# One encoder layer: convolution statistics placed a chunk later, channel sums behind the first key projection, nine gate tiles in the last head pair, and another order of the first output products

## The chip, the cores and the metric

The program runs on one core of one Trainium2 chip. The metric is the device time of one execution in microseconds (us); the median of several runs is compared. The core has TensorE (PE, matrix products), VectorE (DVE), ScalarE (ACT), GpSimd (POOL) and SyncE (SP, which issues most DMAs). Each engine works through its own list of instructions in order and waits on semaphores for what another engine or a DMA has to finish first. TensorE's clock is granted at one of two levels, 1.2 or 2.4 GHz; a granted clock of 0.50 in a view is the lower one.

## The reference, cut to what matters

All inputs are fp32; the width D is 1024. There are 16 meta tokens, 512 prompt tokens and 1024 sample tokens. The two batches are computed together, 1536 tokens beside the meta tokens.

```python
def encoder_layer(h, ...):                 # h: (1, 16 + T, 1024)
    u = rms_norm(h, pre_g)
    z = einsum('bld,de->ble', u, w_in)     # 7 x 1024 output columns
    c_val, c_glu, c_gate, q, k, v, a_gate = split(z)
    conv_out = conv_module(c_val, c_glu, ...) * silu(c_gate)
    o_meta, o_grid = neighbourhood_attention(q, k, v, ..., rel_bias)   # 16 heads of 64
    att = concatenate([o_meta, o_grid]) * silu(a_gate)
    mixed = concatenate([conv_out, att], axis=-1)                      # 2048 channels
    y = einsum('ble,ed->bld', mixed, w_out)
    return h + rms_norm(y, post_g)

def conv_module(val, glu_gate, conv_w, conv_b, ln_g, ln_b):
    u = val * sigmoid(glu_gate)
    y = depthwise_conv(u, conv_w)          # 31 taps along the tokens, per channel
    y = layer_norm(y + conv_b, ln_g, ln_b) # over the 1024 channels of a token
    return silu(y)
```

## The kernel before, in words

**Products.** Every fp32 product is made of three: an operand is split into a high part and the remainder (`whi`, `wlo` for weights, `uw` tiles for tokens), and each contraction chunk gives hi·hi, lo·hi and hi·lo. A projection of 128 output channels over 512 tokens (`proj`, L179) is one PSUM tile of 24 matmuls. A weight block is loaded by SP, cast on ACT (L140) and subtracted on POOL (L141), one block ahead of its use.

**Order.** The program is written as one stream; a scheduler in the framework then sets the order on each engine, by its own simulated times, and pools of buffers add waits. Within an engine that order is fixed.

**Stages.** First the pre-norm with its transposes. Then the convolution stage: the 1024 channels are eight chunks of 128. For chunk c, ACT makes the sigmoid of the glu tiles (L237), DVE multiplies the value tiles into `ub` (L254; one of the two buffers `ub0`, `ub1`), three small copies on POOL (L249, L260, L261) fill the 15-column edges between the token segments, ACT makes the first tap (L267: bias and one scaled copy), and DVE adds the other 30 taps (`conv_taps`, L269), each over 128 x 1536. Chunk 0's taps are made segment by segment as its tokens arrive. From chunk 0 a pivot `m0` per token is taken (`conv_mean`, three ones-matmuls at L279). The statistics of a chunk (`conv_stats`, three parts of 512 tokens) are: `zc` = z - m0 on DVE (L286), its square `zq` on ACT (L291, one buffer), and two running sums on POOL, `acc` (L292) and `accsq` (L293). The centred `zc` goes to DRAM.

**What TensorE does meanwhile.** The table `FILL` gives, per chunk, the fill units beside the next chunk's glu and value tiles: `v` is one unit of value projection (24 matmuls of 256 columns), `c3` or `a1` three tiles of a convolution or attention gate (`c_gate`, `a_gate`; each evacuated by an ACT copy to `ag`, L352, and stored). `TAP_US` is the time that the code allots to a tap when it interleaves the two streams of code, `TAP_MEAN` the tap of chunk 1 behind which `conv_mean` is coded.

**After the convolution.** Six ones-matmuls (L460) sum `acc` and `accsq` over the channels into `std` in DRAM; each result passes through an ACT copy (L462). Then `pair_proj(0)` (four tiles of keys, evacuated on ACT and DVE, L519 to L528) and `pair_q(0,0)`. `e_build` loads the bias tables and adds the masks on POOL (L541). Eight head pairs follow, each in six groups: scores (L602), softmax, transposes (L624), weighted values (L640). `between` puts a projection between two groups; in the last pair, which has no next pair to project for, it takes gate tiles of pairs 4 and 5. Behind the last pair stand the six tiles of `a_gate(6, 7)`.

**Output.** `mix(t, part)` builds the normalized, gated operand of 128 tokens (part 0 convolution, part 1 attention) from DRAM: loads `mb`, `mx`, `gt`, DVE and ACT arithmetic (on ACT a table load, the root L744, eight scaled silus L760, the gate's silu L761, the cast L763). `load_wo(n)` loads and splits block n of 16 of the output weights. The products `py` (L781) of the first two token tiles run side by side over n, then ten more tiles one by one.

## Time and profile before

| what | us |
|---|---|
| runs | 1496.85, 1497.6, 1500.35 |
| median | 1497.6 |
| the profiled execution | 1499.63 |
| its span, first to last instruction | 1497.9 |
| granted clock of TensorE, mean | 0.983 |

The span runs from the first instruction to the last; the execution's time has 1.73 us more around it. Stages in the profile's clock: pre-norm and first projections to about 80, convolution stage to 655, sums and first keys to 696, eight pairs to 1185, the last gates to 1220, output projection to the end.

### The profile page before, as it was taken

The page shows a single profiled execution, that of the slowest core. Times are in us where ns is not written, and L with a number is a line of the kernel's source. Part 1 is how long each engine was busy: PE and PEld are TensorE (multiplying, and loading weights), DVE is VectorE, ACT ScalarE, POOL GpSimd, SP SyncE. Part 2 cuts the span into 40 slices and gives each one's busy share as a digit, 9 for nine tenths or more (in the row PEclk, how much of TensorE's full clock was granted, in tenths as well). Part 3 has the DMA queues.
Part 4 walks back from the last instruction along what each step waited for, and adds up shares of the span by engine and source line. Part 5 has one row for each costly group of instructions (what it writes and reads, how often), then busy time and mean ns, then how long its engine had stood idle before and what let it go on. Part 6 is the DMA issues. An engine that isn't in the chain of part 4 may idle for free.

```text
span 1497.9 us, 24017 instructions
## 1 busy us (share of the span) xinstructions
PE 1450.2 (97%) x9506; PEld 1244.1 (83%) x9506; DVE 1008.5 (67%) x1707; ACT 592.6 (40%) x1297; POOL 339.7 (23%) x260
## 2 busy tenths in 40 slices
PE   7999799999999998989999999999999889999998
PEld 6988698898998887868888888888888668888886
DVE  7599999898989898943555566555555572634341
ACT  7312111212111211123554455555555584566650
POOL 1034351514231414141211111111111001221220
PEclk9999899999999999999999999999999699999999
DMA  8113231222222122232122222122222592545441
GB/s 275 28 42 86 65 92 43 86 79 74 91 82 63 63 83 63 93 100 57 59 61 72 67 72 73 48 73 64 76 76 70 162 305 83 163 145 172 126 136 43
DMA packets 124469, 138.90 MB, mean 93 GB/s; under 512 B 8110, under 2 KB 96430, under 8 KB 124356
## 3 DMA queue, kind: packets, MB, share of 16 engines
q1 hardware_dynamic: 124356, 137.36, 30.0%
q8 instruction: 74, 1.21, 0.4%
q14 instruction: 39, 0.32, 0.1%
HBM read 99.05 MB, written 42.71 MB: 95 GB/s over the span
## 4 chain that ended last, share of the span: by engine, by line
PE 50%; DVE 22%; POOL 3%; DMA 2%; ACT 2%; issue 2%; SPq 0%; DVEq 0%; ACTq 0%; POOLq 0%
DVE z L269 21%; PE mm L179 20%; PE py L781 18%; PE ss L602 5%; PE po L640 4%; PE tp L624 3%; POOL acc L292 2%; DMA mx<-zs 1%; DMA wraw<-in_wo 1%; POOL accsq L293 1%; ACT z L267 1%; ACT mx L760 0%; POOL wlo L141 0%; DMA cgd<-ag 0%; DVE zc L286 0%
## 5 line engine op out<-in xcount | busy, mean ns | idle before, releaser
L179 PE MATMUL mm<-uw,whi 128*128 128x512 f32 (+2 forms) x1888 | 548.4, 370 | 2.6 <-ACT ag L462 1.6
L269 DVE SCALAR_TENSOR_TENSOR z<-ub,cw_sb,z 128x1536 f32<-128x1536 f32 (+2 forms) x270 | 513.4, 1913 | 39.3 <-ACT z L267 31.5
L179 PEld LDWEIGHTS mm<-uw,whi 128*128 128x128 f32 x1888 | 340.0, 190 | 59.7 <-ACT ag L462 3.1
L179 PE MATMUL mm<-uw,wlo 128*128 128x512 f32 (+2 forms) x944 | 348.2, 369 | 2.9 <-POOL wlo L141 2.9
L141 POOL TENSOR_TENSOR wlo<-wraw,whi 128x1024 fp32r<-128x1024 f32 x48 | 134.2, 2797 | 388.8 <-ACT whi L140 374.1
L179 PEld LDWEIGHTS mm<-uw,wlo 128*128 128x128 f32 x944 | 179.3, 190 | 29.5 <-POOL wlo L141 3.3
L781 PE MATMUL py<-uw,mh 128*128 128x512 f32 x576 | 178.6, 391 | 0.0
L179 PE MATMUL tp<-uw,whi 128*128 128x512 f32 (+2 forms) x528 | 142.0, 352 | 0.0
L781 PEld LDWEIGHTS py<-uw,mh 128*128 128x128 f32 x576 | 108.1, 188 | 23.5
L613 ACT ACTIVATE pt<-pt,sm 128x216 f32<-128x216 f32 (+4 forms) x192 | 97.3, 507 | 73.5 <-DVE sm L612 71.9
L781 PE MATMUL py<-uw,ml 128*128 128x512 f32 x288 | 112.6, 391 | 0.0
L764 POOL TENSOR_TENSOR ml<-mx,mh 128x1024 fp32r<-128x1024 f32 x20 | 50.5, 2540 | 241.7 <-ACT mh L763 241.7
L179 PEld LDWEIGHTS tp<-uw,whi 128*128 128x128 f32 x528 | 93.3, 188 | 13.6
L626 ACT COPY pT<-tp 108x256 f32<-108x256 f32 (+4 forms) x192 | 79.3, 423 | 63.6 <-PE tp L624 55.2
L609 DVE CUSTOM_DVE_ANT_0 pt<-ss,ei 128x216 f32<-128x216 f32 (+2 forms) x144 | 62.6, 438 | 59.9 <-PE ss L602 46.4
L179 PE MATMUL tp<-uw,wlo 128*128 128x512 f32 (+2 forms) x264 | 93.0, 352 | 0.0
L624 PE MATMUL tp<-ident,pt 128*96 128x128 f32 (+2 forms) x480 | 89.3, 281 | 1.2 <-ACT pT L626 0.9
L757 DVE TENSOR_TENSOR mx<-mx,mb 128x1024 f32<-128x1024 f32 x12 | 14.7, 1224 | 107.3 <-DMA mx<-zs 107.3
L291 ACT ACTIVATE zq<-zc 128x512 f32<-128x512 f32 x24 | 15.2, 632 | 177.3 <-DVE zc L286 131.8
L332 PE MATMUL mm<-vh,uw 128*128 128x256 f32 x448 | 83.9, 284 | 0.8 <-ACT uw L204 0.6
L615 DVE TENSOR_SCALAR pt<-pt,sm 128x216 f32<-128x216 f32 (+4 forms) x192 | 79.9, 418 | 5.4
L614 DVE RECIPROCAL sm<-sm 128x1 f32<-128x1 f32 x192 | 31.3, 163 | 69.4 <-ACT pt L613 66.8
(184 smaller groups left out, 2335.3 us busy)
## 6 DMA issues: line engine op xcount, KB each, us to landing
wraw<-in_w_main SPq DMA_DIRECT2D x48, 512.0 KB
xt<-in_xn SPq DMA_DIRECT2D x12, 512.0 KB
vd<-vs SPq DMA_DIRECT2D x96, 64.0 KB
zs<-zc SPq DMA_DIRECT2D x24, 256.0 KB
...
```

The costliest lines, as they stand in the source:

```text
L141: eng.tensor_tensor(out=lo, in0=raw, in1=hi.bitcast(F32), op=ALU.subtract)
L179: last_mm[0] = nc.tensor.matmul(ps[:, :n], lhsT=w[:, dc, :], rhs=u[dc // 4][:, dc % 4, :], start=(dc == 0 and i == 0), stop=(dc == DC - 1 ...
L269: nc.vector.scalar_tensor_tensor(out=zv, in0=ub[:, a:b, k:k + 512], scalar=cw_sb[:, c, k:k + 1], in1=zv, op0=ALU.mult, op1=ALU.add)
L332: nc.tensor.matmul(ps[:, :256], lhsT=u[dc // 4][:, dc % 4, :], rhs=w[dc // 4][:, dc % 4, :], start=(dc == 0 and i == 0), stop=(dc == DC - ...
L602: last_qk[0] = nc.tensor.matmul(ss[:, :nk * w], lhsT=q[:, jj].rearrange("p h x -> p (h x)"), rhs=k[:, b0:b0 + nk, ra:ra + rn, :].rearrange ...
L609: nc.vector.tensor_tensor_reduce(out=pv.rearrange("p (k x) -> p k x", k=nk), in0=sv_, in1=e.rearrange("p k r c -> p k (r c)"), scale=1.0, ...
L613: last[0] = nc.scalar.activation(out=pv, in_=pv, func=AF.Exp, bias=sm[:, 1:2], scale=1.0, accum_out=sm[:, 2:3])
L615: nc.vector.tensor_scalar(out=pv, in0=pv, scalar1=sm[:, 3:4], scalar2=None, op0=ALU.mult)
L624: nc.tensor.transpose(out=tp[:kt, k * 128:k * 128 + 128], in_=pv[:, k * kt:k * kt + kt], identity=ident)
L626: nc.scalar.copy(out=pT[:kt, :nt * 128], in_=tp[:kt, :nt * 128])
L640: last_pv[0] = nc.tensor.matmul(po[hs, j, :], lhsT=v, rhs=pT[:kt, k * 128 + h * 64:k * 128 + h * 64 + 64], start=(k == 0), stop=(k == nt - ...
L781: nc.tensor.matmul(pss[hf], lhsT=m[e // 8][:, e % 8], rhs=w[e][:, hf * 512:hf * 512 + 512], start=(n == 0 and i == 0), stop=(n == 15 and i ...
```

## The change

1. `FILL` is dealt out anew: chunk 0's stretch gets five `v` units, later ones seven rather than eight, and the attention gate `a3` leaves the convolution stage. `TAP_US` becomes 2.3 and `TAP_MEAN` 14.
2. The statistics of chunk c-1 are coded behind taps 4, 8 and 12 of chunk c (for c = 1 behind taps 17, 21 and 25). Those of chunk 7 are coded behind its taps, with their sums on DVE.
3. The three edge copies of `ub` go from POOL to ACT.
4. The six channel sums (now L538) are coded behind `pair_proj(0)` and `pair_q(0,0)` and use the `ss` and `tp` banks; the pools and memsets that need the space of the convolution move with them.
5. `between` of the last pair takes nine gate tiles (`a3`, `a4`, `a5`) rather than six.
6. In the output part `mix(0,(1,))`, `mix(1,(0,))` and `mix(1,(1,))` are coded behind weight blocks 5, 7 and 9, the second of them held behind the last gate copy. The first two token tiles multiply the convolution half (n = 0 to 7) of tile 0, then of tile 1, then the attention halves.

```diff
-TAP_US = 1.85
-TAP_MEAN = 6
+TAP_US = 2.3
+TAP_MEAN = 14
-FILL = ("", "v5 c0 v3", "v8 c1", "v1 c2 v7", "v5 c3 v3", "v8 c4", "v1 c5 c6", "a0 a1 a2 a3 c7")
+FILL = ("v5", "c0 v7", "v5 c1 v2", "v7 c2", "v3 c3 v4", "v7 c4", "v1 c5 c6", "a0 a1 a2 c7")
...
-                nc.gpsimd.tensor_copy(out=ub[:, 1, 527:542], in_=ub[:, 2, 15:30])
-                nc.gpsimd.tensor_copy(out=ub[:, 2, 0:15], in_=ub[:, 1, 512:527])
+                nc.scalar.copy(out=ub[:, 1, 527:542], in_=ub[:, 2, 15:30])
+                nc.scalar.copy(out=ub[:, 2, 0:15], in_=ub[:, 1, 512:527])
...
+        first = TAP_MEAN + 3 if c == 1 else 4
         for k, _ in enumerate(conv_taps(c, z, 0, 3)):
             yield TAP_US
             if c == 1 and k == TAP_MEAN:
                 with tc.issue_after(last_mm[0]):
                     conv_mean(zprev[0])
-            if c == 1 and k == TAP_MEAN + 3:
-                for i in range(3):
-                    conv_stats(0, zprev[0], i, nc.gpsimd)
-                    yield TAP_US / 3
-        for i in range(3):
-            conv_stats(c, z, i, nc.gpsimd)
-            yield TAP_US / 3
+            if k in (first, first + 4, first + 8):
+                conv_stats(c - 1, zprev[0], (k - first) // 4, nc.gpsimd)
+                yield TAP_US / 3
+        if c == 7:
+            for i in range(3):
+                conv_stats(c, z, i, nc.vector)
...
+    for _ in pair_proj(0):
+        pass
+    pair_q(0, 0)
     for i in range(3):
         sl = slice(i * 512, i * 512 + 512)
         for k, src in enumerate((acc, accsq)):
-            ps = new_mm()
+            pool, tag = ((ps_s, "ss"), (ps_t, "tp"))[k]
+            ps = pool.tile([128, 512], F32, name=tag, tag=tag)
...
-        for p in (4, 5):
+        for p in (3, 4, 5):
             yield from a_gate(p)
...
         elif p == NPAIR - 1:
-            next(rest, None)
+            for _ in range(1 if i == 1 else 2):
+                next(rest)
...
+        if n == len(groups) + 1:
+            next(rest)
         if n >= 2:
             with tc.issue_after(last_qk[0].ins):
                 weighted(*groups[n - 2])
+        if n == len(groups):
+            next(rest)
...
     for n in range(16):
-        if n == 2:
-            mix(1, (0,))
+        if n == 6:
             mix(0, (1,))
+        elif n == 8:
+            with tc.issue_after(last_copy[0]):
+                mix(1, (0,))
+        elif n == 10:
             mix(1, (1,))
         load_wo(n)
...
-    for n in range(16):
+    for part in range(2):
         for t in range(2):
-            for hf in range(2):
-                product(t, together[t], n, hf)
+            for n in range(part * 8, part * 8 + 8):
+                for hf in range(2):
+                    product(t, together[t], n, hf)
```

**ScalarE between chunk 2 and chunk 3.** A row is a line, an operation and its tiles (`sg` the sigmoid, `zq` the squares, `z` the first tap, `vh` and `whi` casts of weights). Before:

```order
L237 ACTIVATE sg_2351<-tp 128x512
L140 CAST whi<-wraw 128x1024
L291 ACTIVATE zq<-zc 128x512 x3
L267 ACTIVATE z<-ub_129,cb_sb,cw_sb 128x1536
L140 CAST vh<-wraw 128x1024
```

In the changed kernel, at the same boundary (lines are shifted by one):

```order
L140 CAST whi<-wraw 128x1024
L250 COPY ub_129<-ub_129 128x15
L292 ACTIVATE zq<-zc 128x512
L262 COPY ub_129<-ub_129 128x15
L292 ACTIVATE zq<-zc 128x512 x2
L140 CAST whi<-wraw 128x1024
L261 COPY ub_129<-ub_129 128x15
L268 ACTIVATE z<-ub_129,cb_sb,cw_sb 128x1536
```

The three squares still stand ahead of the first tap (L267, now L268), and the edge copies stand among them. So it is also at the boundary from chunk 4 to 5; at the other four, the third square stands behind the first tap, as here from chunk 3 to 4:

```order
L250 COPY ub_128<-ub_128 128x15
L262 COPY ub_128<-ub_128 128x15
L292 ACTIVATE zq<-zc 128x512 x2
L261 COPY ub_128<-ub_128 128x15
L268 ACTIVATE z<-ub_128,cb_sb,cw_sb 128x1536
L292 ACTIVATE zq<-zc 128x512
```

**VectorE at the end of the convolution stage.** `kl` and `ql` are the low parts of keys and queries. Before:

```order
L254 TENSOR_TENSOR ub_129<-tp,sg_4724 128x8x8x8
L269 SCALAR_TENSOR_TENSOR z<-ub_129,cw_sb,z 128x1536 x30
L286 TENSOR_TENSOR zc<-z,m_987 128x512 x3
L520 TENSOR_TENSOR kl<-mm,kh 128x8x8 x2
L528 TENSOR_TENSOR kl<-mm,kh 128x4x64 x2
```

Now:

```order
L287 TENSOR_TENSOR zc<-z,m_987 128x512 x3
L255 TENSOR_TENSOR ub_129<-tp,sg_4718 128x8x8x8
L270 SCALAR_TENSOR_TENSOR z<-ub_129,cw_sb,z 128x1536 x30
L287 TENSOR_TENSOR zc<-z,m_987 128x512 x3
L293 TENSOR_TENSOR acc<-acc,zc 128x512 x2
L294 TENSOR_TENSOR accsq<-accsq,zq 128x512
L293 TENSOR_TENSOR acc<-acc,zc 128x512
L294 TENSOR_TENSOR accsq<-accsq,zq 128x512
L498 TENSOR_TENSOR kl<-mm,kh 128x8x8
L294 TENSOR_TENSOR accsq<-accsq,zq 128x512
L498 TENSOR_TENSOR kl<-mm,kh 128x8x8
L506 TENSOR_TENSOR kl<-mm,kh 128x4x64 x2
```

The evacuation of the first key tiles (L498, L506) stands behind the taps of chunk 7 and all its sums but the last. The 30 taps are still one unbroken run: the `zc` of chunk 6 were coded among them, and the scheduler put them ahead, where they stood before; it does so with the statistics of chunks 1 to 5 too.

**ScalarE around the last gate copy.** `uw`, `whi` are places that the output weights' high parts take, `mh0` to `mh2` the high parts of the mixed operand. Before:

```order
L352 COPY ag_11994<-mm_11969 128x512
L732 CAST uw_12161<-wraw_12159 128x1024
L760 ACTIVATE mx_12041<-mx_12041,lb_sb_97,lg_sb_96 128x128 x8
L732 CAST uw_12166<-wraw_12164 128x1024
L352 COPY ag_12022<-mm_11997 128x512
L763 CAST mh2_12056<-mx2_12049 128x1024
```

Now:

```order
L353 COPY ag_11994<-mm_11969 128x512
L744 CAST uw_12160<-wraw_12158 128x1024
L744 CAST uw_12171<-xr_12169 128x1024
L744 CAST uw_12176<-yo_12174 128x1024
L353 COPY ag_12022<-mm_11997 128x512
L756 ACT_TABLE_LOAD
L756 ACTIVATE mb_12044<-mb_12044,eps_sb_89 128x128
```

The last gate copy stood behind the eight silus of `mix(1,(0,))` and one weight cast; now it stands behind three weight casts, and that `mix` follows it.

## Rows read from the trace of the kernel before

**Rows 1.** The page's first lines: the span, and each engine's busy time, share of the span and instructions.

```profile
span 1497.9 us, 24017 instructions
PE 1450.2 (97%) x9506; PEld 1244.1 (83%) x9506; DVE 1008.5 (67%) x1707; ACT 592.6 (40%) x1297; POOL 339.7 (23%) x260
```

**Rows 2.** The page's 40 slices of 37.4 us: busy tenths of PE, and the clock granted to TensorE in tenths.

```profile
PE   7999799999999998989999999999999889999998
PEclk9999899999999999999999999999999699999999
```

**Rows 3.** The page's chain of work that ended last: shares of the span by engine, then by line.

```profile
PE 50%; DVE 22%; POOL 3%; DMA 2%; ACT 2%; issue 2%; SPq 0%; DVEq 0%; ACTq 0%; POOLq 0%
DVE z L269 21%; PE mm L179 20%; PE py L781 18%; PE ss L602 5%; PE po L640 4%; PE tp L624 3%; POOL acc L292 2%; DMA mx<-zs 1%; DMA wraw<-in_wo 1%; POOL accsq L293 1%; ACT z L267 1%; ACT mx L760 0%; POOL wlo L141 0%; DMA cgd<-ag 0%; DVE zc L286 0%
```

**Rows 4.** Waits of PE, and one of DVE: who waits, for whom, us in total, times, the longest.

```profile
PE ss L279 <- DVE z L269: 8.0, 1, 8.0
PE py L781 <- ACT ag L352: 5.7, 1, 5.7
...
DVE z L269 <- ACT z L267: 31.5, 6, 7.1
```

**Rows 5.** Timeline of DVE between chunk 2 and chunk 3: start, length, instruction, and in brackets the idle time before it and who ended it.

```profile
273.74 1.81 DVE L269 SCALAR_TENSOR_TENSOR z<-ub,cw_sb,z 128x1536 f32<-128x1536 f32 x1
275.64 3.00 DVE L286 TENSOR_TENSOR zc<-z,m 128x512 f32<-128x512 f32 x3
278.56 1.28 DVE L254 TENSOR_TENSOR ub<-mm,sg 128x512 f32<-128x512 f32 x2
286.00 17.27 DVE L269 SCALAR_TENSOR_TENSOR z<-ub,cw_sb,z 128x1536 f32<-128x1536 f32 x5 [6.17 <-ACT z L267]
```

**Rows 6.** Timeline of POOL there.

```profile
276.41 3.38 POOL L292 TENSOR_TENSOR acc<-acc,zc 128x512 f32<-128x512 f32 x2 [6.57 <-DVE zc L286]
279.75 1.29 POOL L293 TENSOR_TENSOR accsq<-accsq,zq 128x512 f32<-128x512 f32 x1
281.00 1.29 POOL L292 TENSOR_TENSOR acc<-acc,zc 128x512 f32<-128x512 f32 x1
282.24 0.20 POOL L261 COPY ub<-ub 128x15 f32<-128x15 f32 x1
282.39 1.28 POOL L293 TENSOR_TENSOR accsq<-accsq,zq 128x512 f32<-128x512 f32 x1
```

**Rows 7.** Timeline of ACT there.

```profile
276.42 0.63 ACT L291 ACTIVATE zq<-zc 128x512 f32<-128x512 f32 x1 [17.96 <-DVE zc L286]
281.07 0.63 ACT L291 ACTIVATE zq<-zc 128x512 f32<-128x512 f32 x1 [4.02 <-POOL accsq L293]
283.70 0.63 ACT L291 ACTIVATE zq<-zc 128x512 f32<-128x512 f32 x1 [1.99 <-POOL accsq L293]
284.24 1.66 ACT L267 ACTIVATE z<-ub,cb_sb,cw_sb 128x1536 f32<-128x1536 f32 x1
```

**Rows 8.** Taps beside POOL: timeline of DVE and of POOL between chunk 1 and chunk 2, and one piece of the chain of waits, in chunk 3, beside a subtraction of POOL's L141.

```profile
210.75 15.77 DVE L269 SCALAR_TENSOR_TENSOR z<-ub,cw_sb,z 128x1536 f32<-128x1536 f32 x6
208.60 6.15 POOL L292 TENSOR_TENSOR acc<-acc,zc 128x512 f32<-128x512 f32 x3
299.44 3.85 DVE z L269
```

**Rows 9.** Timeline of PE behind its wait for a weight block, and of ACT at two gate tiles that follow each other at the full clock.

```profile
586.33 0.79 PE L179 MATMUL mm<-uw,wlo 128*128 128x512 f32 x1 [2.95 <-POOL wlo L141]
600.11 0.59 ACT L352 COPY ag<-tp 128x512 f32<-128x512 f32 x1 [4.88 <-PE tp L179]
605.55 0.59 ACT L352 COPY ag<-tp 128x512 f32<-128x512 f32 x1 [4.85 <-PE tp L179]
```

**Rows 10.** The end of the convolution stage: timelines of DVE (the last two taps, the `zc` of chunk 7; and a lone `zc` of chunk 0), POOL (the last sum) and PE (the first score).

```profile
645.03 3.67 DVE L269 SCALAR_TENSOR_TENSOR z<-ub,cw_sb,z 128x1536 f32<-128x1536 f32 x2
648.73 2.99 DVE L286 TENSOR_TENSOR zc<-z,m 128x512 f32<-128x512 f32 x3
137.65 0.68 DVE L286 TENSOR_TENSOR zc<-z,m 128x512 f32<-128x512 f32 x1
659.62 1.26 POOL L293 TENSOR_TENSOR accsq<-accsq,zq 128x512 f32<-128x512 f32 x1 [0.74 <-ACT zq L291]
695.76 0.29 PE L602 MATMUL ss<-kh,qh 128*128 128x264 f32 x1
```

**Rows 11.** Two of the sums on PE (line's instructions: duration in ns min/median/max, first and last start; a sum is two matmul records).

```profile
L460 PE MATMUL tp<-acc,ones x2: 592/592/592, 656.5 to 657.0; 128*1 128x512 f32 x2
```

**Rows 12.** Busy time by stretch: the stretch, its length, busy time of PE, PEld, DVE, ACT and POOL, the granted clock, the DMA share and GB/s. The last pair's end and the stretch before the first output products.

```profile
1162.00:1166.00 4.00, 1.95 (x13) 1.58 (x13) 1.78 (x9) 1.38 (x4) 0.00 (x0) 0.94 1.11 313
1166.00:1189.20 23.20, 18.72 (x165) 14.75 (x164) 12.62 (x32) 18.97 (x35) 0.00 (x0) 0.50 0.21 69
1219.00:1226.00 7.00, 1.27 (x6) 0.73 (x5) 5.57 (x6) 5.64 (x12) 0.00 (x0) 0.83 1.03 380
1226.00:1230.00 4.00, 4.00 (x10) 3.13 (x11) 2.66 (x5) 3.39 (x4) 0.00 (x0) 0.50 1.01 287
```

**Rows 13.** Timeline of ACT: the silus of `mix` in the last pair and ahead of the last gate copy.

```profile
1178.30 3.18 ACT L760 ACTIVATE mx<-mx,lb_sb,lg_sb 128x128 f32<-128x128 f32 x8
1220.46 3.18 ACT L760 ACTIVATE mx<-mx,lb_sb,lg_sb 128x128 f32<-128x128 f32 x8 [0.72 <-DVE mx L758]
```

More of the change, by code (lines that the diff above doesn't have):

```diff
@@ L73, in _plan @@
         seq += [32 + p, 24 + p]
-    return chunks, seq + [40 + p for p in range(4, NPAIR)]
+    return chunks, seq + [40 + p for p in range(3, NPAIR)]
 CONV_ORDER = tuple((k, i) for k in "gv" for i in range(4))
@@ L218, in tile_encoder @@
     es1 = ExitStack()
-    vpool = es1.enter_context(tc.tile_pool(name="vpool", bufs=1, side="right", reuse_waits="tile"))
+    es1v = ExitStack()
+    vpool = es1v.enter_context(tc.tile_pool(name="vpool", bufs=1, side="right", reuse_waits="tile"))
     cpool = es1.enter_context(tc.tile_pool(name="cpool", bufs=1, reuse_waits="tile"))
@@ L248, in value @@
                     nc.vector.tensor_tensor(out=ub[:, 0, 0:15], in0=psv[:, 1:16], in1=sg[:, 1:16], op=ALU.mult)
-                    nc.gpsimd.tensor_copy(out=ub[:, 1, 0:15], in_=ub[:, 0, 0:15])
+                    nc.scalar.copy(out=ub[:, 1, 0:15], in_=ub[:, 0, 0:15])
                     continue
@@ L351, in gates @@
                 gt = gpool.tile([128, 512], F32, name="ag", tag="ag", bufs=2)
-                nc.scalar.copy(out=gt, in_=ps)
+                last_copy[0] = nc.scalar.copy(out=gt, in_=ps).ins
                 nc.sync.dma_start(dst[g][c], gt)
@@ L453, in tile_encoder @@
             pass
-    for i in range(3):
-        sl = slice(i * 512, i * 512 + 512)
-        for k, src in enumerate((acc, accsq)):
-            ps = new_mm()
-            nc.tensor.matmul(ps[0:1], lhsT=ones[:, 0:1], rhs=src[:, sl], start=True, stop=True)
-            row = gpool.tile([128, 512], F32, name="ag", tag="ag", bufs=2)
-            nc.scalar.copy(out=row[0:1], in_=ps[0:1])
-            nc.sync.dma_start(std[k:k + 1, sl], row[0:1])
-    es1.close()
+    es1v.close()
     banks[:] = 0, ((ps_mm, "mm"),)
     es2 = ExitStack()
-    apool = es2.enter_context(tc.tile_pool(name="apool", bufs=1, reuse_waits="tile"))
     kpool = es2.enter_context(tc.tile_pool(name="kpool", bufs=1, side="right", reuse_waits="tile"))
@@ L473, in tile_encoder, with new_qb @@
     qbs = []
-    for i in range(3):
-        pool = qpool if i < 2 else apool
+    def new_qb(pool):
+        i = len(qbs)
         qh = pool.tile([128, 4, 2, 64], F32R, name=f"qh{i}")
@@ L481, in tile_encoder @@
         qbs.append((qh, ql))
[L482 to L497 removed]
+    for _ in range(2):
+        new_qb(qpool)
     qcount = [0]
@@ L562, in pair_q, with e_build @@
             qbuf[p, g, hf] = qh, ql
+    for _ in pair_proj(0):
+        pass
+    pair_q(0, 0)
+    for i in range(3):
+        sl = slice(i * 512, i * 512 + 512)
+        for k, src in enumerate((acc, accsq)):
+            pool, tag = ((ps_s, "ss"), (ps_t, "tp"))[k]
+            ps = pool.tile([128, 512], F32, name=tag, tag=tag)
+            nc.tensor.matmul(ps[0:1], lhsT=ones[:, 0:1], rhs=src[:, sl], start=True, stop=True)
+            row = gpool.tile([128, 512], F32, name="ag", tag="ag", bufs=2)
+            nc.scalar.copy(out=row[0:1], in_=ps[0:1])
+            nc.sync.dma_start(std[k:k + 1, sl], row[0:1])
+    es1.close()
+    apool = es2.enter_context(tc.tile_pool(name="apool", bufs=1, reuse_waits="tile"))
+    new_qb(apool)
+    ebufs = []
+    for g in range(3):
+        R, mr = GR[g]["R"], META_ROW[g]
+        ei = apool.tile([128, 3, R, 8], F32, name=f"ei{g}")
+        ne = 3 if g == 0 else 2
+        e0 = apool.tile([128, ne, R, 8], F32, name=f"e0{g}")
+        e7 = apool.tile([128, ne, R, 8], F32, name=f"e7{g}")
+        nc.gpsimd.memset(ei[:, 0:2, mr, :], 0.0)
+        nc.gpsimd.memset(ei[:, 2, mr, :], NEG)
+        k7 = ne - 2
+        nc.gpsimd.memset(e0[:, 0:2, mr, :], 0.0)
+        nc.gpsimd.memset(e7[:, k7:k7 + 2, mr, :], 0.0)
+        if g == 0:
+            nc.gpsimd.memset(e0[:, 2], NEG)
+            nc.gpsimd.memset(e7[:, 0], NEG)
+        ebufs.append((ei, e0, e7))
+    def e_build(p):
+        for var in range(3):
+            raw = apool.tile([128, 15, 24], F32, name="raw", bufs=2)
+            nc.sync.dma_start(raw.rearrange("p i c -> p (i c)"), ed[var, 2 * p:2 * p + 2].rearrange("h r q n -> (h r q) n"))
+            for g in range(3):
+                r0, n, i0 = GROWS[g]
+                e = ebufs[g][var]
+                nk = 3 if var == 0 else 2
+                msk = rm_sb[:, MASK_OFF[g]:MASK_OFF[g] + n].unsqueeze(1).unsqueeze(3).broadcast_to([128, nk, n, 8])
+                k0 = 1 if g == 0 and var == 2 else 0
+                nc.gpsimd.tensor_tensor(out=e[:, k0:k0 + nk, r0:r0 + n, :],
+                                        in0=raw[:, i0:i0 + n, 0:8 * nk].rearrange("p i (k c) -> p k i c", c=8),
+                                        in1=msk, op=ALU.add)
     vts, pts, pTs, pos = {}, {}, {}, {}
@@ L668, in tile_encoder @@
     e_build(0)
-    for _ in pair_proj(0):
-        pass
-    pair_q(0, 0)
     groups = [(p, g, hf) for p in range(NPAIR) for g in range(3) for hf in range(2)]
@@ L685, in tile_encoder @@
             between(p, g * 2 + hf)
-        elif n == len(groups):
-            for _ in rest:
-                pass
     with tc.issue_after(last_pv[0]):
```

31 lines of the change are left out of this document (1 added, 30 removed).

## The prediction

> **What bounds the kernel now.** First the page's totals: TensorE is busy 97% of a span of 1497.9 us, VectorE 67% [rows 1]. That alone would say that only less TensorE work helps. The slices show that the clock holds at the higher level but for a few places [rows 2]. Then the chain of waits: TensorE carries only half of it; the taps (L269) carry 21% of the span and the products of L179 20% [rows 3]. 21% is some 310 us of a convolution stage of about 575, so in that stage VectorE sets the end and TensorE, whose work there is nearly as long, follows it. Behind that stage TensorE is the bound, and its idle places count in full.
>
> The change touches four places: chunk boundaries, the passage from convolution to attention, the last pair, and the start of the output products. I take them in order, against the profiled execution's own span.
>
> **Chunk boundaries: about 0.** Between two chunks VectorE waits for ACT's first tap: 31.5 us in six waits, 30.6 of them at five boundaries [rows 4]. At one of these, `zc` and the last value tiles end at 279.83 and the taps start at 286.00 [rows 5]. ACT's first tap takes 1.66 us from 284.24, behind the third `zq` [rows 7]; each `zq` waits for POOL's `accsq`, since there is one `zq` buffer [rows 6, 7]. Taking the edge copies off POOL shortens POOL's chain by two pieces of about 0.15 us; what matters is where the first tap stands on ACT, and the order shows that.
> - At four boundaries it now stands behind the second square only. That ends at 281.7; an edge copy of 0.2 (the length on POOL [rows 6]), the first tap at 282.0, taps at 283.9: the stall falls from 6.2 to about 4.1.
> - At two it still stands behind the third square, and behind a weight cast of about 1.05 and a copy as well: third square about 283.5 to 284.2, cast and copy to 285.4, first tap to 287.1. The stall is about 7.3.
>
> Sum: 4 x 4.1 + 2 x 7.3 = 31. Before, it was 30.6 at five boundaries; at the sixth (1 to 2) there was no stall, but the six taps behind it took 15.77 us, 2.63 each, beside POOL's sums [rows 8]. A tap alone takes 1.81 [rows 5], so that boundary paid 6 x 0.82 = 4.9. The same price now falls on the taps which the earlier start puts beside the last one or two sums: 4 boundaries x 1 to 2 x 0.8 = 3 to 6. So 34 to 37 after, 35.5 before. The statistics themselves aren't spread: the order has the three `zc` together at each boundary, as before.
>
> `v5` in chunk 0's stretch puts five units of 2.8 us ahead of chunk 1's value tiles (2.8 is half of a gate tile's 5.44 [rows 9], at 256 of 512 columns). The chain there has chunk 0's remaining taps as cover; I take +1.5 for what sticks out, between 0 and 6. The wait of `conv_mean` (8.0 us of TensorE [rows 4]) moves behind `v` units; TensorE isn't the bound there, so it gives nothing. End of taps: **+1.7** (from -5 to +8).
>
> **From the last tap to the first score: -15.1.** Before, taps end at 648.73 and the first score starts at 695.76: 47.0 us [rows 10]. In it lie the rest of the gate tiles, POOL's sums (last one ending 660.88 [rows 10]), the six sums and the whole of the first projections. Now TensorE has less to do in the convolution stage (three tiles of `a3`, 16.3, are gone), so it reaches `pair_proj(0)` early, fills the three PSUM tiles that it may, and waits for VectorE's evacuation, which is queued behind the sums of chunk 7. From the last tap:
> - three `zc` at 0.62 (a lone one is 0.68 [rows 10], POOL no longer beside), 1.9; six additions of the same shape, about 0.6 each, with two squares of 0.63 [rows 7] and their semaphores in between, and the first evacuations: 7.5 in all (between 6 and 11);
> - 24 matmuls of the fourth key tile, 24 of `pair_q`, 14 of the next tile: 62 x 0.227 (a tile of 24 in 5.44 [rows 9]) = 14.1;
> - six sums = 5.0: one is two records, the second 0.5 us behind the first and 0.59 long [rows 11], so between 0.8 and 1.1 each; I take 0.83, since the modelled ends overlap;
> - half clock after so long an idle time: a wait of 2.95 us for a weight block [rows 9] and the idle time of the last stage [rows 12] were each followed by some microseconds at 1.2 GHz; 4 us at half clock lose 2.0 in the latter. I take 2.8.
>
> Together 29.4. Ten matmuls of the following tile are left for later, +2.5. So 29.4 + 2.5 - 47.0 = -15.1; with +1.7 the attention starts **13.4 earlier**. If TensorE arrives late or VectorE's sums take longer, it is -8; if the squares run without gaps, -18.
>
> **Last pair and gates: +16.3, then -8.** The three tiles of `a3` come back here at 5.44 each [rows 9]. Here TensorE is the bound, and its idle time is a place to put them: from 1162 to 1166 it is busy 1.95 of 4.00, from 1166 to 1189.2 18.72 of 23.20, at granted clock 0.50 [rows 12]. Idle 2.05 + 4.48 = 6.5, and 18.72 us of work at half clock would be 9.4 at full: 15.9 lost. The nine tiles stand among those steps, so the idle places get filler. But the cause stays: ACT's queue holds eight silus of 3.18 us between two PSUM copies [rows 13], table loads besides, and VectorE waits for DMA there. I expect half of it back, **-8** (from 0, if each gap stays beside the new tiles, to -12.6).
>
> **Start of the output products: -6.3.** Before, `py` waits 5.7 us for the last gate copy, which stands behind eight silus [rows 4, 13]; then 4.00 us at half clock lose 2.0 [rows 12]: 7.7. Now that copy has three weight casts ahead of it, which wait only for their DMAs; the silus follow it. About 1.4 remain (the copy of 0.6 and its semaphores): **-6.3** (from 0 to -7.5). What is late next: the products of the convolution half of tile 0, then 1, need a weight block every 6 matmuls, 1.4 us, where it was every 12; and tile 1's operand, whose chain on ACT (table loads, root, silus, cast) starts only behind the last copy, is needed 8 blocks x 6 = 48 matmuls, 10.9 us, behind the start, or later where the scheduler puts more between.
>
> **Sum.** 1497.9 - 13.4 + 16.3 - 8 - 6.3 = 1486.5. Around the span lie 1.73 us, and the median of the runs is 2.0 under the profiled execution (1497.6 against 1499.63): **1486 us**. Its own range, from the bounds of the terms that can move together, is 1478 to 1494.
>
> **Rivals.**
> - *VectorE is set free.* If the first tap comes well ahead of the sums, as at the boundary 1 to 2 before, the stalls of 31 go. But the taps then run beside POOL's sums and pay 0.8 each [rows 8]: 4.9 per boundary against 4.1 to 7.3. At most some 2 per boundary are won, 12 in all: 1474. Against it speaks ACT's order, with two squares ahead. Chance 0.1.
>   The Trainium skill, "SBUF — State Buffer" (Who interferes with whom), says that of a VectorE operation with two SBUF inputs and a GpSimd one that reads SBUF, the second to issue blocks until the first is done. By this each sum of 1.28 would cost the taps 1.28, six of them 7.7, and there would be nothing to win. The trace shows less, 0.8 per tap beside sums, and 2.0 beside a subtraction of L141 (3.85 against 1.81 [rows 5, 8]).
> - *The output products wait all the same,* for weight blocks or for tile 1's operand, and the last pair gives back only a little: the terms -8 and -6.3 become -3 and -2, and the sum 1496. For it speaks that SP's loads and ACT's casts were the pace of that stretch already (DMA share 1.03 [rows 12]). Chance 0.19.
> - *Slower.* The edge copies on ACT wait for VectorE's value tiles, which stand behind three `zc`; ACT is in order, so all squares behind them wait too, and so do `accsq` and the first tap. At 2 to 3 the value tiles end at 279.83 [rows 5], the first square was at 276.42 [rows 7]: up to 3.4 us later per boundary, 6 x 3.4 = 20, in the stage where VectorE sets the end: 1506. It decides from 2.7 per boundary (16 in all). Against it: at two boundaries a square stands ahead of the copies, and POOL's first two sums need no square and cover some 3 us [rows 6]. Chance 0.14.
> - *It does nothing.* The spread of the statistics already does nothing, by the order. If TensorE's work is all that counts (97% busy [rows 1]), moving three tiles and gaps that come back elsewhere leave 1498. That lies within 0.3%; chance 0.05.
>
> **How the numbers follow.** Forecast 0.52, rivals 0.1, 0.19, 0.14, 0.05. A measurement of this kernel can tell 0.3%, 4.5 us, from no change: faster is under 1493.1, slower over 1502.1. The forecast's case is faster in 9 of 10 (0.47), with rival one 0.57, and a fifth of rival two (0.04): 0.61. Slower: rival three, less a little, and the tails: 0.14. Same: 0.25. For 8 in 10 the range leaves out most of the slower rival and the tail of the first: 1474 to 1502.
>
> **What would show it.** Right: VectorE's waits for L268 still sum to about 30 us; TensorE idles some 10 us ahead of the fourth key tile; first score about 13 us earlier; the stretch of low clock in the last pair is half as long; no wait of `py` over 2 us. Wrong: taps that end over 8 us earlier or later; a wait of `py` in its first 30 us for a weight block or for `mh1`; gate tiles that make the last pair 16 us longer with its low clock as it was.

## The result and the profile after

The changed kernel takes 1490.6 us (median of four runs, 1487.5 to 1491.4) against 1498.4 for the kernel before beside it: a ratio of 0.994 (95% interval 0.992 to 0.996). It is faster, by 7.8 us where 11.6 were forecast, and within the stated range. One of the four executions of e11 below ran in a slower state (2035.3 us at a mean granted clock of 0.654) and is left out of its numbers.

The page's totals and its chain by engine and by line, of the changed kernel:

```profile
span 1489.2 us, 24000 instructions
PE 1444.3 (97%) x9506; PEld 1242.1 (83%) x9506; DVE 1014.3 (68%) x1713; ACT 598.6 (40%) x1323; POOL 321.5 (22%) x230
...
PE 61%; DVE 6%; DMA 1%; ACT 1%; POOL 1%; issue 1%; DVEq 0%; SPq 0%; ACTq 0%
PE mm L179 25%; PE py L796 18%; PE ss L615 5%; DVE z L270 4%; PE po L653 4%; PE tp L637 4%; PE tp L179 3%; PE po L179 2%; DMA wraw<-in_wo 1%; PE mm L333 1%; POOL acc L293 0%; DMA yo<-in_wo 0%; DVE accsq L294 0%; POOL accsq L294 0%; DVE uw L745 0%
```

The totals hardly differ from [rows 1]. The chain does, on its face: the taps fell from 21% [rows 3] to 4%, though they take as long as ever, 511 us in all. Here is the place where the chain passes from TensorE to VectorE, ahead of chunk 7's taps, and VectorE there:

```profile
556.09 10.91 PE tp L179 x48
567.00 5.58 PE po L179 x24
572.58 5.47 PE mm L179 x24
578.24 0.69 DVE zc L287
```

```profile
577.64 0.69 DVE L255 TENSOR_TENSOR ub<-tp,sg 128x512 f32<-128x512 f32 x1
578.24 2.99 DVE L287 TENSOR_TENSOR zc<-z,m 128x512 f32<-128x512 f32 x3
581.15 0.68 DVE L255 TENSOR_TENSOR ub<-tp,sg 128x512 f32<-128x512 f32 x1
```

This link is no wait: VectorE has no gap there. The tiles that end just ahead of it, `po` and `mm`, are gate tiles, which ACT copies at 590.47 and 590.93; what VectorE reads are the `tp` tiles. The last of these, the last value tile, ended at 567.00 and was read 14 us later, as in the kernel before (565.45 and 579.35). So the fall from 21% to 4% does not say who sets the end of the stage. The 11.0 us that TensorE idles at that end, below, do say it: VectorE still sets it.

Waits, the same view as [rows 4]:

```profile
PE mm L179 <- DVE kl L506: 11.0, 1, 11.0
...
PE mm L179 <- POOL wlo L141: 4.0, 2, 3.5
PE po L653 <- ACT pT L639: 2.5, 1, 2.5
PE py L796 <- ACT ag L353: 2.1, 1, 2.1
...
DVE z L270 <- ACT z L268: 31.9, 7, 7.0
```

The new wait of 11.0 us is the one ahead of the fourth key tile. VectorE's stall at the chunk boundaries is unchanged in sum (31.5 before). ACT between chunks 2 and 3, and the first tap of VectorE there and between chunks 3 and 4 [rows 5, 7]:

```profile
284.70 0.63 ACT L292 ACTIVATE zq<-zc 128x512 f32<-128x512 f32 x1 [4.69 <-DVE zc L287]
287.60 0.20 ACT L262 COPY ub<-ub 128x15 f32<-128x15 f32 x1 [2.27 <-DVE ub L255]
289.39 0.63 ACT L292 ACTIVATE zq<-zc 128x512 f32<-128x512 f32 x1 [1.58 <-POOL accsq L294]
291.90 0.63 ACT L292 ACTIVATE zq<-zc 128x512 f32<-128x512 f32 x1 [1.88 <-POOL accsq L294]
292.44 1.03 ACT L140 CAST whi<-wraw 128x1024 fp32r<-128x1024 f32 x1
293.38 0.19 ACT L261 COPY ub<-ub 128x15 f32<-128x15 f32 x1
293.48 1.66 ACT L268 ACTIVATE z<-ub,cb_sb,cw_sb 128x1536 f32<-128x1536 f32 x1
```

```profile
295.18 6.36 DVE L270 SCALAR_TENSOR_TENSOR z<-ub,cw_sb,z 128x1536 f32<-128x1536 f32 x3 [7.02 <-ACT z L268]
...
364.61 1.82 DVE L270 SCALAR_TENSOR_TENSOR z<-ub,cw_sb,z 128x1536 f32<-128x1536 f32 x1 [4.17 <-ACT z L268]
```

The squares wait for POOL's sums, and the first tap stands behind them in ACT's queue. The end of the stage, timelines of VectorE, POOL, and PE [rows 10]:

```profile
650.51 1.90 DVE L287 TENSOR_TENSOR zc<-z,m 128x512 f32<-128x512 f32 x3
652.33 1.29 DVE L293 TENSOR_TENSOR acc<-acc,zc 128x512 f32<-128x512 f32 x2
653.53 2.83 DVE L294 TENSOR_TENSOR accsq<-accsq,zq 128x512 f32<-128x512 f32 x1
656.28 0.68 DVE L293 TENSOR_TENSOR acc<-acc,zc 128x512 f32<-128x512 f32 x1
657.12 0.69 DVE L294 TENSOR_TENSOR accsq<-accsq,zq 128x512 f32<-128x512 f32 x1 [0.17 <-ACT kh L497]
...
659.85 1.46 DVE L506 TENSOR_TENSOR kl<-mm,kh 128x256 fp32r<-128x256 f32 x3 [0.44 <-ACT kh L505]
```

```profile
653.37 2.45 POOL L141 TENSOR_TENSOR wlo<-wraw,whi 128x1024 fp32r<-128x1024 f32 x1 [26.81 <-ACT whi L140]
```

```profile
660.42 0.76 PE L179 MATMUL mm<-uw,whi 128*128 128x512 f32 x1 [11.04 <-DVE kl L506]
...
683.08 0.29 PE L615 MATMUL ss<-kh,qh 128*128 128x264 f32 x1
```

One sum of squares took 2.83 us where its like takes 0.69: POOL's subtraction ran beside it. TensorE came to its wait at 649.38, 1.0 us ahead of the end of the last tap, and went on 10.0 us behind it. Busy time by stretch, columns as in [rows 12]: the wait, the tile behind it, the whole last pair (the same for the kernel before in a fence of its own), and the first products:

```profile
649.40:660.40 11.00, 0.00 (x0) 0.01 (x1) 9.68 (x14) 4.47 (x10) 2.45 (x1) 0.61 0.42 143
660.40:668.40 8.00, 7.98 (x25) 6.41 (x26) 0.90 (x2) 0.18 (x1) 0.00 (x0) 0.68 0.00 0
1101.25:1180.93 79.68, 77.16 (x676) 65.16 (x674) 40.58 (x146) 45.87 (x113) 10.45 (x5) 0.98 0.31 99
1218.00:1222.00 4.00, 4.00 (x12) 3.15 (x11) 2.37 (x3) 3.96 (x5) 0.00 (x0) 0.57 1.02 384
```

```profile
1111.79:1184.94 73.15, 66.61 (x604) 55.68 (x602) 40.35 (x147) 43.52 (x110) 7.66 (x4) 0.87 0.29 87
```

With nine tiles in place of six the last pair is 6.5 us longer, not 16.3: idle time fell from 6.5 to 2.5, and the mean clock rose from 0.87 to 0.98.

The stages of every kernel, read from the timelines (us of the span; e1 to e12 are the experiments below; the first tap is chunk 0's; the last column is the median of its runs, where the kernel before had 1498.4 to 1499.4):

| kernel | first tap | last tap ends | first score | last pair starts | last weighted value | first product | last product | median |
|---|---|---|---|---|---|---|---|---|
| before | 63.6 | 648.7 | 695.8 | 1111.8 | 1184.9 | 1225.9 | 1491.6 | 1498.4 |
| after | 65.4 | 650.4 | 683.1 | 1101.3 | 1180.9 | 1217.7 | 1482.6 | 1490.6 |
| e1 | 65.1 | 647.7 | 679.4 | 1097.6 | 1177.3 | 1210.3 | 1476.8 | 1482.9 |
| e2 | 64.7 | 644.1 | 671.6 | 1089.9 | 1169.5 | 1206.2 | 1471.1 | 1478.9 |
| e3 | 63.7 | 648.2 | 678.9 | 1097.2 | 1176.9 | 1214.5 | 1479.4 | 1488.0 |
| e4 | 63.6 | 648.6 | 686.3 | 1104.5 | 1177.0 | 1211.8 | 1481.1 | 1489.9 |
| e5 | 63.4 | 648.0 | 680.2 | 1098.5 | 1181.4 | 1220.9 | 1486.5 | 1496.4 |
| e6 | 65.0 | 649.9 | 681.9 | 1100.2 | 1180.6 | 1218.4 | 1485.0 | 1491.5 |
| e7 | 64.3 | 649.0 | 682.0 | 1100.3 | 1179.8 | 1215.4 | 1479.5 | 1487.9 |
| e8 | 65.4 | 651.8 | 684.3 | 1102.5 | 1182.3 | 1218.6 | 1483.6 | 1491.8 |
| e9 | 63.6 | 643.0 | 670.6 | 1088.9 | 1167.1 | 1201.0 | 1466.0 | 1475.9 |
| e10 | 64.5 | 647.1 | 679.1 | 1097.4 | 1177.2 | 1212.5 | 1476.0 | 1483.3 |
| e11 | 63.6 | 642.8 | 686.9 | 1105.1 | 1175.7 | 1208.7 | 1480.6 | 1491.2 |
| e12 | 63.6 | 648.0 | 695.3 | 1111.4 | 1184.2 | 1224.1 | 1490.1 | 1498.5 |

The edits of e3 to e7 leave VectorE's work up to the last tap alone, yet the last taps end between 648.0 and 649.9, after's at 650.4. The scatter lies ahead of the first tap; from there to the last tap these six kernels agree to 0.4 us (584.6 to 585.0, and 585.1 before the change). So a column of one profile is known to about 1.2 us either way, and differences between columns are steadier. In what follows, "the passage" is the length from the last tap to the first score.

### The profile page after: what moved, and what is told of

Read it like the earlier page. It is cut to its first block, busy times and chain, and to the rows that moved or that the text cites. A ratio compares the mean times of both kernels' runs of the same rounds, so it can differ in the third digit from the quotient of the medians.

```text
span 1489.2 us, 24000 instructions
## 1 busy us (share of the span) xinstructions
PE 1444.3 (97%) x9506; PEld 1242.1 (83%) x9506; DVE 1014.3 (68%) x1713; ACT 598.6 (40%) x1323; POOL 321.5 (22%) x230
## 4 chain that ended last, share of the span: by engine, by line
PE 61%; DVE 6%; DMA 1%; ACT 1%; POOL 1%; issue 1%; DVEq 0%; SPq 0%; ACTq 0%
PE mm L179 25%; PE py L796 18%; PE ss L615 5%; DVE z L270 4%; PE po L653 4%; PE tp L637 4%; PE tp L179 3%; PE po L179 2%; DMA wraw<-in_wo 1%; PE mm L333 1%; POOL acc L293 0%; DMA yo<-in_wo 0%; DVE accsq L294 0%; POOL accsq L294 0%; DVE uw L745 0%
## 5 line engine op out<-in xcount | busy, mean ns | idle before, releaser
L179 PE MATMUL mm<-uw,whi 128*128 128x512 f32 (+2 forms) x1904 | 559.6, 373 | 11.0 <-DVE kl L506 11.0
L270 DVE SCALAR_TENSOR_TENSOR z<-ub,cw_sb,z 128x1536 f32<-128x1536 f32 (+2 forms) x270 | 511.4, 1901 | 39.9 <-ACT z L268 31.9
L179 PEld LDWEIGHTS mm<-uw,whi 128*128 128x128 f32 x1904 | 344.2, 190 | 70.0 <-issue 13.6
L179 PE MATMUL mm<-uw,wlo 128*128 128x512 f32 (+2 forms) x952 | 354.5, 372 | 4.0 <-POOL wlo L141 4.0
L141 POOL TENSOR_TENSOR wlo<-wraw,whi 128x1024 fp32r<-128x1024 f32 x48 | 126.9, 2645 | 450.4 <-ACT whi L140 440.3
L179 PE MATMUL tp<-uw,whi 128*128 128x512 f32 (+2 forms) x512 | 133.9, 345 | 0.0
L179 PEld LDWEIGHTS tp<-uw,whi 128*128 128x128 f32 x512 | 89.4, 188 | 12.1 <-issue 0.5
L333 PE MATMUL mm<-vh,uw 128*128 128x256 f32 x448 | 87.6, 291 | 7.3 <-ACT vs L336 4.8
L179 PE MATMUL tp<-uw,wlo 128*128 128x512 f32 (+2 forms) x256 | 88.1, 344 | 0.0
L333 PEld LDWEIGHTS mm<-vh,uw 128*128 128x128 f32 x448 | 72.9, 197 | 9.3 <-ACT vs L336 5.4
```

Of the source, the lines that this page charges most:

```text
L141: eng.tensor_tensor(out=lo, in0=raw, in1=hi.bitcast(F32), op=ALU.subtract)
L179: last_mm[0] = nc.tensor.matmul(ps[:, :n], lhsT=w[:, dc, :], rhs=u[dc // 4][:, dc % 4, :], start=(dc == 0 and i == 0), stop=(dc == DC - 1 ...
L270: nc.vector.scalar_tensor_tensor(out=zv, in0=ub[:, a:b, k:k + 512], scalar=cw_sb[:, c, k:k + 1], in1=zv, op0=ALU.mult, op1=ALU.add)
L333: nc.tensor.matmul(ps[:, :256], lhsT=u[dc // 4][:, dc % 4, :], rhs=w[dc // 4][:, dc % 4, :], start=(dc == 0 and i == 0), stop=(dc == DC - ...
```

## The experiments

All ratios are to the kernel before; the changed kernel's is 0.994. "Theory" and "rival" are those of the expectation printed above each result.

**e1: the statistics really spread.**

```diff
-                conv_stats(c - 1, zprev[0], (k - first) // 4, nc.gpsimd)
+                with tc.issue_after(last_tap[0]):
+                    conv_stats(c - 1, zprev[0], (k - first) // 4, nc.gpsimd)
```

Here `last_tap` is the latest tap that was coded.

> The changed kernel, with the three statistics of the chunk before held behind taps 4, 8 and 12 (chunk 0's behind 17, 21, 25), as the change describes them; the order shows them there. Theory (a POOL sum beside taps costs about 0.85 us, and the first tap no longer stands behind squares): VectorE's waits for the first tap fall from 31.9 us to about 15, the three zc of a chunk from 3.0 to 2.0 together, the sums under taps cost 5 per chunk instead of about 2: taps end some 6 us earlier than at 650.4, and the time is 1482 to 1487, limited by TensorE, which ran only 3 us ahead at the last chunk. Rival (a sum blocks the taps for its whole 1.28 us): 7.7 per chunk, taps end about 10 us later, 1498 to 1502.

Ratio 0.989 (0.988 to 0.991), 1482.9 us, in the theory's range. VectorE's waits for the first tap, the taps as a group (busy, mean ns), and POOL's sums:

```profile
DVE z L272 <- ACT z L270: 13.8, 7, 2.3
```

```profile
L272 DVE SCALAR_TENSOR_TENSOR z<-ub,cw_sb,z 128x1536 f32<-128x1536 f32 (+2 forms) x270 | 535.4, 1990 | 21.2 <-ACT z L270 13.8
L296 POOL TENSOR_TENSOR accsq<-accsq,zq 128x512 f32<-128x512 f32 x21 | 58.9, 2805 | 0.0
```

The stall fell by 18 and the taps' busy time rose by 24: 42 sums of seven chunks now run beside them. Stall, `zc` and value tiles between the chunks' taps fell from 56 to 20 us, since the `zc` moved among the taps too, and the seven runs of taps grew by 34. The last tap ends 2.7 earlier (2.4 from the first tap on), the theory's sign and half its size. From the last weighted value to the last product it is 2.2 shorter too; there the products wait 2.6 us for a high part and not for the gate copy. Why this order came out is not shown. The rival, a block for the sum's whole length, falls.

**e2: squares written over z.**

```diff
-        zq = zpool.tile([128, 512], F32, name="zq", bufs=1)
+        zq = z[:, i]
```

> The changed kernel, with the squares written over the finished part of z instead of into the one buffer zq, so that no square waits for POOL's accsq and the first tap does not wait for POOL through the squares. Theory (the stall at the chunk boundary and the contention of taps with POOL's sums are two prices for the same work): waits for the first tap fall from 31.9 to about 15, but four to five sums per boundary run beside taps at 0.8 to 1 us each; end of taps within 4 us of 650.4, time 1488 to 1493. Rival (VectorE is set free by the shorter stall): taps end 12 to 17 us earlier, TensorE sets the end of the stage, 1478 to 1483.

Ratio 0.987 (0.985 to 0.988), 1478.9 us. This is the rival's time, against my theory. VectorE and POOL between chunks 2 and 3, then the waits:

```profile
289.66 11.47 DVE L270 SCALAR_TENSOR_TENSOR z<-ub,cw_sb,z 128x1536 f32<-128x1536 f32 x4 [2.36 <-ACT z L268]
```

```profile
289.73 4.07 POOL L294 TENSOR_TENSOR accsq<-accsq,z 128x512 f32<-128x512 f32 x2
293.75 3.92 POOL L141 TENSOR_TENSOR wlo<-wraw,whi 128x1024 fp32r<-128x1024 f32 x1
```

```profile
PE mm L179 <- POOL wlo L141: 10.2, 3, 6.1
...
PE mm L179 <- DVE kl L506: 0.4, 1, 0.4
...
DVE z L270 <- ACT z L268: 14.5, 7, 2.8
```

The stall fell by 17.4, and the taps' busy time rose only from 511.4 to 523.3, by 11.9; my theory needed about as much as the stall fell. The last tap ends 6.4 earlier (5.7 from the first tap on). Another 5.1 come behind it: the passage takes 27.6 us instead of 32.7, and TensorE waits 0.4 instead of 11.0. Three things make up that wait's end: the last tap ends 6.4 earlier, TensorE comes 1.5 later, and the drain (from the last tap to the fourth key tile) takes 7.3 us instead of 10.0. Of the drain's 2.7, 2.1 are the addition, which POOL's subtraction no longer holds; only the rest can be the squares, which no longer alternate with the sums. Without an idle stretch ahead of it the fourth key tile also runs at full clock. What is late next is POOL: its sums, slowed by the taps, hold a weight's low part for 6.1 us.

**e3: the last sums on POOL.**

```diff
-                conv_stats(c, z, i, nc.vector)
+                conv_stats(c, z, i, nc.gpsimd)
```

> The changed kernel, with the sums of chunk 7 on POOL, as before the change, so that VectorE evacuates the key tiles right behind the last zc. Theory (the 11.0 us wait of TensorE for the fourth key tile is VectorE's queue of six sums): that wait falls to 4 or 5 us, the six channel sums then wait up to 3 us for POOL's last sum, the first score comes 3 to 6 us earlier, time 1485 to 1488. Rival (the channel sums take the place of the wait, POOL's chain ending some 12 us behind the last tap): first score where it was, within 1.5 us, time 1489 to 1492.

Ratio 0.992 (0.991 to 0.994), 1488.0 us, in the theory's range but not separable from the changed kernel. The passage takes 30.7, 1.9 less, below the theory's 3 to 6. TensorE's wait is 8.3, where the theory had 4 to 5. Timeline of ACT ahead of its end:

```profile
653.65 0.63 ACT L292 ACTIVATE zq<-zc 128x512 f32<-128x512 f32 x1 [2.56 <-POOL accsq L294]
654.19 0.20 ACT L497 CAST kh<-mm 128x64 fp32r<-128x64 f32 x1
```

The keys' high parts stand behind a square that waits for POOL, so the alternation of square and sum is there on either engine. The drain takes 7.9 us instead of 10.0. These 2.1 are just what the held addition of the changed kernel cost; here POOL makes both sums and subtraction, one after the other. So moving the sums off VectorE wins that addition back and no more, and the alternation by itself is worth under 1 us (e2's drain is 0.7 shorter). The larger part of the 11.0 us is that the last tap ends late: in e2, where it ends 6.4 earlier, 0.4 are left.

**e4: a3 back in the convolution stage.**

```diff
-FILL = ("v5", "c0 v7", "v5 c1 v2", "v7 c2", "v3 c3 v4", "v7 c4", "v1 c5 c6", "a0 a1 a2 c7")
+FILL = ("v5", "c0 v7", "v5 c1 v2", "v7 c2", "v3 c3 v4", "v7 c4", "v1 c5 c6", "a0 a1 a2 a3 c7")
...
-        for p in (3, 4, 5):
+        for p in (4, 5):
...
```

> The changed kernel, with the three tiles of a3 back behind a2 in the convolution stage, and six gate tiles in the last pair as before the change. Theory (TensorE idles 11.0 us and some half clock ahead of the fourth key tile, so a3 is nearly free there): first score 2 to 4 us later than 683.1, last pair 6 to 7 us shorter than 79.7, time 1486 to 1489. Rival (a3 pays its full 16.3 in the convolution stage): first score 14 to 16 us later, time 1498 to 1502.

Ratio 0.994 (0.992 to 0.995), 1489.9 us. The first score is 3.2 later and the last pair takes 72.4 instead of 79.7, both as the theory has it. The passage shows more, 5.1 longer, since here the first tap was 1.8 earlier. The last pair's mean granted clock is 0.86, close to the 0.87 of the kernel before; with nine tiles it was 0.98. The time misses the theory by 0.9: from the last weighted value to the last product 304.2 instead of 301.7, the products waiting 4.0 us for a high part of tile 1.

**e5: part 6 undone.** The three mixes at n == 2, the products over n side by side, as before.

> The changed kernel, with part 6 undone: mix(1,(0,)), mix(0,(1,)) and mix(1,(1,)) coded behind weight block 1 and the products of the two first tiles side by side over n. Theory (part 6 is what brought the output products forward): from the last weighted value to the end of the last product 305 to 307 us again, where the changed kernel has 301.7 and the kernel before 306.7; time 1494 to 1496. Rival (the earlier start comes from the wider spacing of the last pair, whose gate tiles leave ACT time for the weight casts): 301 to 303, time 1490 to 1492.

Ratio 0.998 (0.997 to 0.999), 1496.4 us, 0.4 over the theory's range; from the last weighted value to the last product it is 305.1, as the theory has it. `PE py` waits 5.0 us for the gate copy. The last pair:

```profile
1098.45:1181.37 82.92, 78.42 (x676) 66.00 (x674) 41.51 (x147) 49.78 (x117) 10.47 (x5) 0.96 0.30 97
```

It is 3.2 longer than the changed kernel's: what I put down to gate tiles alone is also ACT's queue, freed of `mix(1,(0,))`. In e5 a table load of 1.28 us and a root of 0.40 of that `mix` stand ahead of the `pT` copies, and `po` waits 4.2 us for them instead of 2.5; the mean clock is 0.96 instead of 0.98.

**e6: only the products side by side again.**

> The changed kernel, with only the products of the first two tiles side by side over n again; the mixes stay where the change puts them. Theory (the halves matter because tile 1's operand is ready only some 10 us behind the last gate copy): TensorE waits 6 to 10 us for it at the start of the output products; 307 to 311 us from the last weighted value to the last product, time 1496 to 1500. Rival (the scheduler puts products of tile 0 ahead by itself): under 304, time 1489 to 1492.

Ratio 0.994 (0.993 to 0.996), 1491.5 us. From the last weighted value to the last product it is 304.4, 2.7 longer than in the changed kernel's profile, but the times can't be separated. This is the rival's time, with a length between the two. There is no wait of 6 to 10 us: the longest is 3.9 for the gate copy.

**e7: weight casts behind the last gate copy.**

```diff
+        if n > 8:
+            with tc.issue_after(last_copy[0]):
+                load_wo(n)
+        else:
+            load_wo(n)
```

> The changed kernel, with the casts of the output weight blocks from 9 on held behind the last gate copy on ACT. Theory (the first output product's 2.1 us wait and the half clock behind it come from three casts that wait for their DMAs ahead of that copy): the wait falls under 1 us, 298 to 300.5 us from the last weighted value to the last product, time 1487 to 1489.5. Rival (the later casts make the products wait for their blocks instead): a wait of 2 to 5 us for a cast or a low part within 30 us of the first product, time 1490 to 1494.

Ratio 0.992 (0.990 to 0.993), 1487.9 us. From the last weighted value to the last product it is 299.7, and the wait is 0.7: as the theory has it. The interval touches the changed kernel's (0.992 to 0.996), so the gain of 2.7 rests on the wait and the length as well.

**e8: edge copies back on POOL.**

> The changed kernel, with the three edge copies of ub back on POOL. Theory (two copies of 0.15 us in POOL's chain hardly matter; what counts is that squares and sums stand ahead of the first tap): VectorE waits 30 to 36 us for the first tap instead of 31.9, time 1489 to 1493. Rival (the copies on ACT are what let the first tap come earlier at four boundaries): 38 to 45 us of waits, taps end 6 to 12 us later, time 1496 to 1502.

Ratio 0.995 (0.993 to 0.997), 1491.8 us; VectorE waits 32.7. This is the theory: in this kernel part 3 alone changes no time that can be told (from the first tap to the last it is 1.5 us longer).

**e9: e2 and e7 together.**

> The changed kernel with two edits together: the squares written into z (worth 11.7 us alone) and the weight casts from block 9 on behind the last gate copy (worth 2.7 us alone). Theory (the two places are a stage apart and on the path both times): the gains add up, 1475 to 1478. Rival (the earlier attention shifts the weight loads against the last pair, and one gain eats the other): 1478.5 to 1482.

Ratio 0.984 (0.983 to 0.986), 1475.9 us: the gains add, as the theory has it. The step from e2 is again small for the intervals (e2's is 0.985 to 0.988), and shows in the length from the last weighted value to the last product, 298.9 instead of 301.6. This is the fastest version, 23 us under the kernel before.

**e10: e9 with the statistics spread.**

> As the kernel with both edits, and the statistics held behind taps 4, 8 and 12 as well. Theory (spreading costs the taps more contention than it saves at the boundary once the squares no longer wait for POOL, but POOL is free for weight splits there): taps end 1 to 4 us later than without the spread, TensorE's waits for low parts of weights shorter by 4 to 6, time 1475 to 1479. Rival (the spread sums are hidden beside taps): taps end earlier, 1470 to 1474.

Ratio 0.989 (0.988 to 0.990), 1483.3 us, slower than either side said. The taps end 4.0 later than in e9 (3.2 from the first tap on), as expected; the rest is the passage, 32.1 instead of 27.6. VectorE and POOL there:

```profile
650.91 2.83 DVE L295 TENSOR_TENSOR acc<-acc,zc 128x512 f32<-128x512 f32 x1
```

```profile
650.74 2.45 POOL L141 TENSOR_TENSOR wlo<-wraw,whi 128x1024 fp32r<-128x1024 f32 x1 [21.96 <-ACT whi L140]
```

POOL's subtraction held an addition again (2.1 us), TensorE waited 7.8 us, and the stretch of 8 us behind that wait held 25 matmuls at a mean granted clock of 0.70, some 2.4 us lost. These two sizes add up to the 4.5; no run takes them apart. In e9 the same subtraction met VectorE's sums as well, but there it started while one of them ran, and POOL was the one held (3.70 us for it, 0.69 for each sum), and TensorE did not wait.

**e11: e2 with a3 back in the convolution stage.**

> The changed kernel with the squares written into z, and a3 back in the convolution stage with six gate tiles in the last pair. Theory (a3 was nearly free there only because TensorE waited 11 us for the sums of chunk 7; with that wait gone its 16.3 us are paid): first score 12 to 16 us later than in the run with the squares in z alone, last pair 7 us shorter, time 1484 to 1488. Rival (a3's place does not matter, as in the changed kernel): 1477 to 1480.

Ratio 0.994 (0.992 to 0.995), 1491.2 us. The first score is 15.3 later than in e2 (the passage 16.6 longer) and the last pair takes 70.6, 9.1 less: the theory's mechanism. The time is 3 over its range, and the products wait for tile 1:

```profile
PE py L794 <- ACT mh L773: 6.7, 1, 6.7
```

**e12: the kernel before, squares over z.**

> The kernel before the change, with nothing changed but the squares written into z. Theory (the stall at the chunk boundaries is a price of VectorE's chain in both kernels, but behind the taps the kernel before is held by TensorE, its gate tiles lasting to 655): taps end 5 to 8 us earlier than 648.7, first score 2 to 6 us earlier than 695.8, time 1493 to 1497. Rival (the stall alone is what holds the kernel, whatever the change did): 1486 to 1489.

Ratio 1.000 (0.998 to 1.000), 1498.5 us: no change. Both sides fall, for the stall itself stayed, 32.5 us. POOL and ACT between chunks 2 and 3:

```profile
283.73 0.20 POOL L261 COPY ub<-ub 128x15 f32<-128x15 f32 x1
```

```profile
283.96 1.68 ACT L267 ACTIVATE z<-ub,cb_sb,cw_sb 128x1536 f32<-128x1536 f32 x1 [4.41 <-POOL ub L261]
```

With the squares out of the way the first tap waits for an edge copy that stands in POOL's queue behind five sums. Two waits of nearly the same length lay side by side; removing either alone (e8 against after, e12 against before) shows nothing, removing both (e2) shows 17 us of stall.

## Why the prediction was right, and where it was off

- **Chunk boundaries, about 0: right, and the end of the taps right by luck.** Stalls of 31 at six boundaries were forecast and 31.1 measured (0.9 of the 31.9 lie in chunk 0): 7.0 at the two long boundaries, where 7.3 was forecast, and 3.6 to 5.1 at the four short ones, where it was 4.1. Read off ACT's order, that held. The end of the taps at +1.7 is another matter. Its parts add up to +1.5, all of it from `v5`, and from the first tap to the last the two kernels take 585.1 and 585.0: `v5` cost nothing. The 1.7 that was measured lies ahead of the first tap, in the scatter.
- **From last tap to first score, 29.4: the term that was mis-sized.** It measured 32.7. The drain of 7.5 took 10.0 (650.4 to 660.4), 2.1 of it from one addition beside POOL's subtraction. I left that out, though POOL made the same subtraction right behind the taps in the kernel before (at 655.3). The tile behind it ran half-clocked as forecast: 8.0 us in place of 5.4. With the work left for later the attention gained 10.5 us (last pair's start) instead of 13.4.
- **Last pair, +16.3 - 8: right in sign, better in size.** It measured +6.5 instead of +8.3. Nine tiles in the old output order (e5) cost 9.8, and part 6, which I had credited to the output products only, took 3.2 of that away. That the tiles fill the idle places is shown by e4: with six tiles the clock stays at 0.86. The stretch of low clock all but went, where I had it halved.
- **Output products, -6.3: they gave -5.0** (306.7 to 301.7). The products still waited 2.1 us for the gate copy, just over the 2 named as a sign; it stood behind casts that wait for their DMAs, and some half clock followed (0.57 over 4 us), which the forecast took as gone. e7 shows 2.0 more to be had.
- **Together** -10.5 + 6.5 - 5.0 = -9.0 against -11.4, and the span is 8.7 shorter.
- **The rivals.** "VectorE is set free" was priced at 12 us at most. e2 gained nearly that, 11.7 below the changed kernel, but close to half of it in the passage and not at the boundaries. The price per tap that I took, 0.8 beside a sum, held (0.9, below). What was too high was the number of taps that pay it: in e2 two or three per boundary, not six, since the other sums are done before the first tap starts. The slower rival did not happen: in ACT's timeline above the edge copy waits 2.27 us for VectorE, and the square behind it waits for POOL 1.58 us more: POOL's first sums cover the copy. The rule of the Trainium skill, "SBUF — State Buffer" (Who interferes with whom), a block for the whole length, would have made e1 slower; it was faster. But in single pairs (2.83 us for an addition beside 2.45 of POOL) the loser was held for nearly all of it, as the rule has it.
- **What the parts are worth.** Of the 7.8 us, e5 puts 5.8 on part 6. Part 3 (e8) and `a3`'s place (e4) change the time by about 1 us or less, and the last sums on VectorE rather than POOL (e3) gain nothing. Parts 1 and 4 and the later place of the statistics were never undone alone. So it is measured that the passage fell from 47.1 to 32.7, 5.1 of it by `a3`'s leaving (e4), but how the rest divides is not shown.
